# Phase one of a streaming hybrid layer: sigmoids held behind PSUM exits, z copied out of PSUM, B and C in a tile of their own

## The chip, the core and the metric

The kernel runs on one core of a Trainium2 chip, as one launch. The metric is the device time of an execution in microseconds; lower is better. The core has a matrix engine (PE, TensorE; its weight load is shown as PEld), a vector engine (DVE, VectorE), a scalar engine (ACT, ScalarE), a general one (POOL, GpSimd) and a queue that issues most DMAs (SP, SyncE). They run side by side, each in its own fixed order, and wait for each other through semaphores. Matmuls write into PSUM; the other engines read it from there, and a PSUM bank can only be written anew when its readers are done.

## What is computed

One inference step of one layer, for 2048 prompt tokens and 32 tokens of a running stream. The mixer reads a normalised input through one projection: half of its heads are stick-breaking attention, the other half a Mamba-2 SSD. Then come an output projection and a feed-forward network with a short convolution. The change is in the SSD side of the projection. Cut to that part:

```
# x: normalised input, 1024 wide; proj gives q, k, v (512 each), z (512), xBC (768), dt (8)
xBC, tail = causal_dwconv(xBC, prev, w, bias)      # 4 taps, 768 channels: x 512, B 128, C 128
xBC = xBC * sigmoid(xBC)                           # SiLU
y = ssd_scan(x, softplus(dt + b), a, B, C, h0) + D * x
y = rmsnorm(y * z * sigmoid(z), g)                 # gate, then norm
```

## The kernel before

Everything up to about 645 us is `phase_in`, which is called phase one here. It takes the tokens in four stretches `s` = 0 to 3 (512, 512, 512 and 544 tokens; the last one has the 32 stream tokens) and works with channels on the partitions. All projections are float32 products made of three matmuls: each operand is split in a high and a low half (`xhi`, `xlo`; a weight `w` is cast to its high half by ScalarE, L145, and GpSimd makes the low half, L146), and `dense` (L161) multiplies high by high, low by high and high by low for eight pieces of the input: 24 matmuls for a tile of 128 channels and up to 512 tokens. In s = 3 such a tile is two halves of 272 tokens. The results land in a PSUM tile `o` from a pool of two banks, which all projections of the phase share. So while one tile is being multiplied, the tile before it must be read out of the other bank, and a late exit stops TensorE.

One stretch runs like this:

- `split`: x, already scaled, gives `xhi` (ScalarE, L319) and `xlo` (VectorE, L320).
- Six convolution tiles `c` in the order 4 (B), 5 (C), 0, 1, 2, 3 (x). Each: 24 matmuls, a ScalarE copy from PSUM to `raw` (L377, L379 for the stream tokens), four VectorE operations (L384 and three times L388) into `xc`, a ScalarE sigmoid `t` (L392) and a VectorE product (L393). `xc` has one buffer, so this stretch's convolution can't start before the stretch before it is done with its own `xc`.
- The v tiles (L412): tokens in blocks of 128, for each block two halves of 24 matmuls with 260 columns, and a ScalarE copy out of each (L421; L419 in s = 0).
- Softplus and the SSD in blocks of 128 tokens: mask and decay in `acB` (VectorE, L488, L510; ScalarE exp, L492), the products with it on TensorE (L538), states `hT` (L562). B and C are operands of TensorE there (`cbm` comes from their product).
- `prep(s + 1)`: squares of the next x (ScalarE, L303 and L306; sums on GpSimd), its rstd (L248), and eight products on VectorE (L310), which scale it. k and q tiles.
- `gate`: four z tiles. In s = 1 and 2 a sigmoid `t` is read straight from PSUM (L627), VectorE multiplies PSUM by it (L628), which frees the bank, and multiplies `xc` by that (L630). In s = 0 a VectorE copy is made first; in s = 3 the gate runs later, spread over the attention.
- `gate_norm`: squares of `xc` (L641, L644), a sum over channels by a matmul `st` (L177), square root (ScalarE, L180), reciprocal (VectorE, L183), four products (L650), and the halves of the result, `khi` (ScalarE, L654) and `klo` (GpSimd, L656), which two DMAs each write out (L657, L658). The last `klo` is the last reader of `xc`.

No one writes the order of the engines by hand. The program is written in the order above, and a scheduler with a timeline of its own sets each engine's order from the dependencies, so an edit in one place can reorder its surroundings. Phase two is attention with the output projection, phase three the feed-forward network; the diff does not touch their code.

Of the kernel before, what the change touches and what calls it, by code (L numbers as in the profile page):

```python
# [8 lines left out]
F32 = mybir.dt.float32  # L9
F32R = mybir.dt.float32r  # L10
BF16 = mybir.dt.bfloat16
AF = mybir.ActivationFunctionType
ALU = mybir.AluOpType
# [18 lines left out]
P = 128  # L32
# [13 lines left out]
NSB = len(SBS)  # L46
# [19 lines left out]
def tiles_of(n):  # L66
    return [(0, n)] if n <= 512 else [(0, n // 2), (n // 2, n)]


class Kernel:  # L70
# [5 lines left out]
    def pin(self, mm):  # L76

        if self.anchor is not None:
            self.tc.add_manual_dep(
                mm.ins, self.anchor,  # L80
                mybir.DependencyInfo(mybir.DependencyClass.NoSync, mybir.DependencyReason.DATA),
                reason="pin",
            )

    def mark(self, mm):
        self.anchor = mm.ins.name
# [166 lines left out]
def phase_in(kn, ctx):  # L253
    nc, tc, a, o = kn.nc, kn.tc, kn.a, kn.o
# [5 lines left out]
    tmp = pool("in_tmp", 2)  # L260
# [94 lines left out]
    for s, (t0, nt) in enumerate(SBS):  # L355
        last = s == NSB - 1
        if s == 0:
            xs, r0 = first()
            rcol = kn.rcol
# [1 line left out]
            xs = split(s, nxt)  # L361
        xhi, xlo = xs
        raw = ep.tile([P, 6, 550], F32, name="raw")
        xc = kn.xcp.tile([P, 6, 547], F32, name="xc")
        W = 547 if last else 512
        nc.vector.tensor_copy(raw[:, :, 0:3], hist[:])
        if last:
            nc.vector.tensor_copy(
                raw[:, :, 515:518], kn.cv[:, C_SST : C_SST + 18].rearrange("p (c t) -> p c t", t=3)
            )  # L370
        for c in (4, 5, 0, 1, 2, 3):
            w = wfirst if s == 0 and c == 4 else kn.weight(wp, a["wbx"][c])
            for c0, c1 in tiles_of(nt):
                ps = psd.tile([P, 512], F32, name="o")
                kn.dense(ps, w, xs, c0, c1)
                e = min(c1, 512)
                nc.scalar.copy(raw[:, c, 3 + c0 : 3 + e], ps[:, : e - c0])  # L377
                if c1 > 512:
                    nc.scalar.copy(raw[:, c, 518:550], ps[:, e - c0 : c1 - c0])  # L379
            if s == 0:  # L380
                nc.vector.tensor_tensor(raw[:, c, 3 : 3 + nt], raw[:, c, 3 : 3 + nt], r0[:, :nt], op=ALU.mult)
            y = xc[:, c, :W]
            wc = C_SW + c * 4
            nc.vector.tensor_scalar(  # L384
                y, raw[:, c, 0:W], kn.col(wc), kn.col(C_SB + c), op0=ALU.mult, op1=ALU.add
            )
            for i in range(1, 4):
                nc.vector.scalar_tensor_tensor(  # L388
                    y, raw[:, c, i : i + W], kn.col(wc + i), y, op0=ALU.mult, op1=ALU.add
                )  # L390
            t = tmp.tile([P, 550], F32, name="t")
            nc.scalar.activation(t[:, :W], y, AF.Sigmoid)  # L392
            nc.vector.tensor_tensor(y, y, t[:, :W], op=ALU.mult)  # L393
        if last:
            nc.sync.dma_start(o["sconv"][0], raw[:, :, 512:515])
            nc.sync.dma_start(o["sconv"][1], raw[:, :, 547:550])
# [9 lines left out]
        for b in range(nb):  # L406
            q = min(P, nt - b * P)
            vp = [psd.tile([P, 512], F32, name="o") for _ in range(2)]
            for h in range(2):
                for k in range(KC):  # L410
                    for i, (l, rr) in enumerate(((xhi, wv[0]), (xlo, wv[0]), (xhi, wv[1]))):
                        nc.tensor.matmul(  # L412
                            vp[h][:q, :260], l[k][:, b * P : b * P + q], rr[:, k, h * 260 : h * 260 + 260],
                            start=i == 0 and k == 0, stop=i == 2 and k == KC - 1,
                        )
            v = sd.tile([P, 520], F32, name="v")
            for dst, src in ((v[:q, 0:260], vp[0][:q, :260]), (v[:q, 260:520], vp[1][:q, :260])):
                if s == 0:
                    nc.scalar.activation(dst, src, AF.Copy, scale=rcol[:q, b : b + 1])  # L419
                else:  # L420
                    nc.scalar.copy(dst, src)  # L421
            nc.vector.tensor_tensor(
                u[:q, b * 8 : b * 8 + 8], v[:q, 512:520], kn.cv[:q, C_DTB : C_DTB + 8], op=ALU.add
            )
            tok = t0 + b * P
            nc.sync.dma_start(o["v"][tok : tok + q, :], v[:q, :512])
            if b == 4:
                nc.sync.dma_start(kn.vF[:], v[:DEC, :512])
                continue
            vs = sd.tile([P, 2, 512], F32R, name="vs", bufs=1)  # L430
            nc.gpsimd.tensor_copy(vs[:, 0, :], v[:, :512])
            nc.gpsimd.tensor_tensor(vs[:, 1, :], v[:, :512], vs[:, 0, :].bitcast(F32), op=ALU.subtract)
            for e in range(2):
                nc.sync.dma_start(
                    kn.vS[s][:, :, b, e * DH : e * DH + DH].rearrange("h p d -> p h d"),
                    vs[:, e, :].bitcast(F32).rearrange("p (h d) -> p h d", d=DH),
                )
# [17 lines left out]
        ps = psm.tile([P, 512], F32, name="st")  # L455
# [10 lines left out]
        ps = psm.tile([P, 512], F32, name="st")  # L466
# [6 lines left out]
        for b in range(nb):  # L473
            q = min(P, nt - b * P)
            col0 = 515 if b == 4 else b * P
            sl = slice(col0, col0 + q)
# [17 lines left out]
            h_in = hS if b == 4 else hT[state["h"]]  # L494
            cy = psy.tile([P, 2, 512], F32, name="y")
            for g in range(2):
                rows = slice(g * 64, g * 64 + 64)
                nc.tensor.matmul(cy[:q, g, :q], xc[rows, 4, sl], xc[rows, 5, sl], start=True, stop=True)
                for i in range(2):
                    nc.tensor.matmul(  # L500
                        cy[:, g, P + i * q : P + i * q + q],
                        h_in[rows, 2 * i : 2 * i + 2, :].rearrange("p h d -> p (h d)"), xc[rows, 5, sl],
                        start=True, stop=True,
                    )
            cbm = sd.tile([P, 2, P], F32, name="cbm")
# [13 lines left out]
            ps = psm.tile([P, 512], F32, name="st")  # L519
# [9 lines left out]
                xw[:q], xdt[:q], te[:q, b * 8 : b * 8 + 8].unsqueeze(2).to_broadcast([q, NH, DH]), op=ALU.mult  # L529
            )  # L530
            ps = psm.tile([P, 512], F32, name="st")
            nc.tensor.transpose(ps[:q, :P], xc[:, 4, sl], kn.ident[:])
            bT = sd.tile([P, P], F32, name="bT")
            nc.scalar.copy(bT[:q, :], ps[:q, :P])
            yt = psy.tile([P, 2, 512], F32, name="y")
# [12 lines left out]
            ps = psm.tile([P, 512], F32, name="st")  # L548
# [6 lines left out]
            for g in range(2):  # L555
                rows = slice(g * 64, g * 64 + 64)
# [16 lines left out]
        for name, dst in (("wk", kn.kS), ("wq", kn.qS)):  # L573
            for c in range(4):
# [4 lines left out]
                for c0, c1 in tiles_of(nt):  # L579
                    ps = psd.tile([P, 512], F32, name="o")  # L580
                    kn.dense(ps, w, xs, c0, c1)
                    n = c1 - c0
# [13 lines left out]
        if last:  # L596
            return lambda tm, pool: (
                gate(kn, s, xs, xc, None, tm),
                gate_norm(kn, s, xc, tm, lambda sq, *r: kn.rstd_narrow(pool, *kn.bank, [sq], *r)),
            )  # L600
        bufs = {"khi": 2, "klo": 2, "t": 2, "sq": 1}
        tm = lambda nm: (so if nm in ("khi", "klo") else tmp).tile([P, 550 if nm == "t" else 544], F32, name=nm, bufs=bufs[nm])
        for _ in gate(kn, s, xs, xc, r0 if s == 0 else None, tm):
            pass
# [4 lines left out]
def gate(kn, s, xs, xc, r0, tm):  # L609

    nc, nt = kn.nc, SBS[s][1]
    tiles = tiles_of(nt)
    for c in range(4):
        w = kn.weight(kn.wp, kn.a["wz"][c])
        for c0, c1 in tiles:
            n = c1 - c0
            ps = kn.po.tile([P, 512], F32, name="o")
            for k in range(KC):
                kn.dense(ps, w[k : k + 1], xs, c0, c1, k0=k, first=k == 0, last=k == KC - 1, pin=s == NSB - 1)
                if len(tiles) == 1 or k % 2:  # L620
                    yield
            t = tm("t")
            if r0 is not None:
                z = tm("t")
                nc.vector.tensor_tensor(z[:, :n], ps[:, :n], r0[:, c0:c1], op=ALU.mult)
                ps = z
            nc.scalar.activation(t[:, :n], ps[:, :n], AF.Sigmoid)  # L627
            nc.vector.tensor_tensor(t[:, :n], ps[:, :n], t[:, :n], op=ALU.mult)  # L628
            e = min(c1, 512)
            nc.vector.tensor_tensor(xc[:, c, c0:e], xc[:, c, c0:e], t[:, : e - c0], op=ALU.mult)  # L630
            if c1 > 512:
                nc.gpsimd.tensor_tensor(xc[:, c, 512:544], xc[:, c, 515:547], t[:, e - c0 : n], op=ALU.mult)
# [839 lines left out]
def build(nc, tc, a, o):  # L1472
    kn = Kernel(nc, tc, a, o)
    with ExitStack() as ctx:
# [17 lines left out]
        with ExitStack() as c2:  # L1492
            kn.wp, kn.unit, kn.wbufs, kn.rbufs = c2.enter_context(tc.tile_pool(name="weights_in", bufs=1)), KC, 2, 2
            rest = phase_in(kn, c2)
# [125 lines left out]
```

## Time and profile before

| | |
|---|---|
| time, median of 3 runs | 2935.15 us (2931.43 to 2939.62) |
| profiled execution | 2941.02 us |
| its span | 2939.2 us, 46252 instructions |
| granted TensorE clock | 0.982 |
| busy | TensorE 96%, VectorE 58%, ScalarE 43%, GpSimd 43% |
| TensorE busy in 0 to 650 us | 593.75 us |

The span is the profiled part of the execution; 1.8 us lie around it. A busy share is an average over phases: what an edit in phase one can be worth is read from TensorE's waits there. In a row of the timeline the numbers are the start and the length in us, then engine, line, operation, output and inputs; the bracket at its end is the idle time before it and what ended it. In a row of groups they are the busy sum in us and the mean of one in ns.

### The profile page before, as it was taken

The numbers are of one execution on the slowest core, as the hardware profiler recorded it, in microseconds if no ns is written. First come the engines' busy times: TensorE is split into PE (matmuls) and PEld (weight loads), VectorE is DVE, ScalarE is ACT, GpSimd is POOL, SyncE is SP. The second block draws the span as 40 slices with busy tenths as digits, with TensorE's granted clock in tenths as the row PEclk, the third lists the DMA queues.
The fourth block names the chain that finished last, engine by engine and source line by source line (L and its number), as shares of the span: only waits on it lengthen the run. The fifth ranks groups of instructions, "written<-read, shape, count | busy, mean of one in ns | idle before, by whom it ended". The sixth has DMA issues, their size and how long they took to land.

```text
span 2939.2 us, 46252 instructions
## 1 busy us (share of the span) xinstructions
PE 2814.1 (96%) x16771; PEld 2427.5 (83%) x16771; DVE 1690.8 (58%) x2628; ACT 1263.4 (43%) x2622; POOL 1275.4 (43%) x1131
## 2 busy tenths in 40 slices
PE   7999999989889999999999999999999999999997
PEld 6777777977788888897788888977888889999997
DVE  7667586566773555447555556675666653623333
ACT  4344444337665555446333444654444443321111
POOL 4565555435766666656322323453223233511113
PEclk9999999989999999999999999999999999999999
DMA  5646464648787778777655556656555445765556
GB/s 179 183 137 193 132 176 124 174 115 271 247 282 263 253 263 276 266 256 250 215 180 172 174 180 219 225 182 205 176 172 170 160 159 202 241 181 179 170 178 200
DMA packets 333093, 586.47 MB, mean 200 GB/s; under 512 B 73306, under 2 KB 192738, under 8 KB 332866
## 3 DMA queue, kind: packets, MB, share of 16 engines
q1 hardware_dynamic: 332866, 583.52, 62.1%
q8 instruction: 134, 2.20, 0.3%
q14 instruction: 93, 0.76, 0.1%
HBM read 445.70 MB, written 137.69 MB: 198 GB/s over the span
## 4 chain that ended last, share of the span: by engine, by line
PE 72%; DVE 13%; DMA 7%; ACT 3%; issue 2%; POOL 1%; SPq 1%; DVEq 0%; ACTq 0%; POOLq 0%
PE o L161 35%; PE u L161 12%; PE t L161 10%; PE z L863 4%; PE pa L904 4%; PE pt L882 3%; DVE xc L388 2%; DMA acB<-acD 2%; PE o L412 1%; DVE acB L488 1%; DVE prow L714 1%; DMA xr<-hS 1%; DVE xc L384 1%; DVE xlo L320 1%; DVE x L310 1%
## 5 line engine op out<-in xcount | busy, mean ns | idle before, releaser
L161 PE MATMUL o<-xhi,w 128*128 128x512 f32 (+2 forms) x3968 | 1047.9, 346 | 24.1 <-ACT xhi L334 8.0
L161 PEld LDWEIGHTS o<-xhi,w 128*128 128x128 f32 x3968 | 697.3, 191 | 119.0 <-ACT xhi L334 8.0
L161 PE MATMUL o<-xlo,w 128*128 128x512 f32 (+2 forms) x1984 | 683.8, 345 | 6.3 <-DVE xlo L320 4.2
L146 POOL TENSOR_TENSOR w<-wraw,w 128x512 fp32r<-128x512 f32 (+3 forms) x244 | 384.3, 1577 | 261.4 <-ACT w L145 232.2
L719 POOL TENSOR_TENSOR beta<-beta,prow 128x512 f32<-128x512 f32 (+3 forms) x256 | 252.5, 987 | 442.7 <-DVE prow L714 366.8
L161 PEld LDWEIGHTS o<-xlo,w 128*128 128x128 f32 x1984 | 380.0, 192 | 50.4 <-DVE xlo L320 6.1
L161 PE MATMUL u<-xhi,w 128*128 128x512 f32 x1056 | 350.3, 398 | 0.0
L161 PE MATMUL o<-ah,w 128*128 128x512 f32 x992 | 344.4, 403 | 4.3 <-DVE f L1348 3.8
L1300 POOL TENSOR_TENSOR y<-y,gb 128x512 f32<-128x512 f32 (+1 forms) x88 | 116.0, 1318 | 503.2 <-ACT gb L1299 503.1
L714 DVE TENSOR_TENSOR_SCAN prow<-gam,prow,z 128x513 f32<-128x513 f32 x192 | 245.2, 1278 | 74.1 <-ACT beta L712 69.7
L887 DVE TENSOR_TENSOR wt<-pt,wt 128x512 fp32r<-128x512 f32 (+2 forms) x320 | 191.0, 602 | 159.6 <-ACT wt L886 157.8
L886 ACT CAST wt<-pt 128x512 fp32r<-128x512 f32 (+2 forms) x320 | 166.9, 527 | 218.2 <-PE pt L882 216.3
L145 ACT CAST w<-wraw 128x512 fp32r<-128x512 f32 (+3 forms) x244 | 172.1, 705 | 170.6 <-PE o L161 98.6
L161 PEld LDWEIGHTS u<-xhi,w 128*128 128x128 f32 x1056 | 199.1, 189 | 46.8
L161 PEld LDWEIGHTS o<-ah,w 128*128 128x128 f32 x992 | 187.2, 189 | 47.0 <-DVE f L1348 6.0
L711 ACT ACTIVATE gam<-z 128x512 f32<-128x512 f32 (+2 forms) x320 | 172.3, 538 | 96.0 <-PE z L863 53.9
L161 PE MATMUL u<-xlo,w 128*128 128x512 f32 x528 | 209.5, 397 | 0.0
L161 PE MATMUL o<-al,w 128*128 128x512 f32 x496 | 196.7, 397 | 0.0
L161 PE MATMUL t<-xhi,w 128*128 128x272 f32 x960 | 189.6, 293 | 2.6 <-DMA w<-wS_up 1.7
L882 PE MATMUL pt<-ident,beta 128*128 128x128 f32 x1088 | 180.3, 277 | 4.2 <-DVE wt L887 2.7
L1292 DVE SCALAR_TENSOR_TENSOR y<-gb,cv,y 128x512 f32<-128x512 f32 (+1 forms) x176 | 142.4, 809 | 72.6 <-ACT y L1290 69.9
L904 PE MATMUL pa<-wt,v 128*64 128x256 f32 (+3 forms) x1152 | 172.3, 280 | 8.6 <-DVE wt L887 6.6
(275 smaller groups left out, 4956.4 us busy)
## 6 DMA issues: line engine op xcount, KB each, us to landing
w<-wS_up SPq DMA_DIRECT2D x264, 512.0 KB, 3.6
w<-wS_dn SPq DMA_DIRECT2D x144, 384.0 KB, 3.5
wS_up<-w SPq DMA_DIRECT2D x88, 512.0 KB, 3.4
w<-wS_out SPq DMA_DIRECT2D x78, 512.0 KB, 5.7
wraw<-wup SPq DMA_DIRECT2D x88, 256.0 KB, 4.0
k<-kS SPq DMA_DIRECT2D x80, 256.0 KB, 4.1
v<-vS SPq DMA_DIRECT2D x80, 256.0 KB, 3.8
wS_dn<-w SPq DMA_DIRECT2D x48, 384.0 KB, 3.1
```

What stands on the lines that cost most here:

```text
L145: nc.scalar.copy(hi, raw[:, :m, :])
L146: nc.gpsimd.tensor_tensor(lo, raw[:, :m, :], hi.bitcast(F32), op=ALU.subtract)
L161: mm = nc.tensor.matmul(ps[:, : c1 - c0], l, r, start=first and i == 0 and k == 0, stop=last and i == 2 and k == len(w) - 1, **({"skip_gro ...
L711: nc.scalar.activation(g[:, c0:512], z, AF.Sigmoid, scale=-0.125)
L714: nc.vector.tensor_tensor_scan(back(pr), back(g), z[:, 0:1].to_broadcast([P, n + 1]), self.kn.ones[:, 0:1] if prev is None else prev, op0= ...
L719: eng.tensor_tensor(b[:, :n], b[:, :n], pr[:, c0 + 1 : 513], op=ALU.mult)
L863: mm = nc.tensor.matmul(z[:, :n], q[:, P * b : P * b + P], k[:, :n], start=e == 0, stop=e == 1 and kc < s)
L882: mm = nc.tensor.transpose(t[:, P * j : P * j + P], w[:, P * j : P * j + P], kn.ident[:])
L886: nc.scalar.copy(hi, t)
L887: nc.vector.tensor_tensor(lo, t, hi.bitcast(F32), op=ALU.subtract)
L904: nc.tensor.matmul(av[:m, 2 * P * p + c0 : 2 * P * p + 2 * P], v[:, j, :m], wt[:, rest, j, c0:], start=kc == s and p + j + rest == 0, stop ...
L1292: nc.vector.scalar_tensor_tensor(y[:, :W], gb[:, i : i + W], kn.col(wc + i), y[:, :W], op0=ALU.mult, op1=ALU.add)
```

## The change

Lines in the new kernel are 8 to 22 higher. There are three edits, all in phase one.

1. A helper `behind` adds a dependency that sets order alone, without a semaphore. The sigmoid and product of a convolution tile are no longer issued with it but owed, and put behind the PSUM copy of the next tile; those of the last tile (c = 3) behind the v copy of block 0.
2. In s = 1 and 2 z is copied from PSUM into a new tile `zc` (two buffers) by ScalarE. Sigmoid and product read `zc`: eight more ScalarE copies.
3. B and C go into a tile `bc` of their own with its own buffer; `xc` keeps the four x tiles.

```diff
+    def behind(self, inst, other):
+        self.tc.add_manual_dep(
+            inst.ins, other.ins.name,
+            mybir.DependencyInfo(mybir.DependencyClass.NoSync, mybir.DependencyReason.DATA),
+            reason="behind",
+        )
...
-        xc = kn.xcp.tile([P, 6, 547], F32, name="xc")
+        xc = kn.xcp.tile([P, 4, 547], F32, name="xc")
+        bc = kn.xcp.tile([P, 2, 547], F32, name="bc")
...
+        owed = None
+        def silu(y, copy):
+            t = tmp.tile([P, 550], F32, name="t")
+            kn.behind(nc.scalar.activation(t[:, :W], y, AF.Sigmoid), copy)
+            nc.vector.tensor_tensor(y, y, t[:, :W], op=ALU.mult)
...
-            y = xc[:, c, :W]
+            y = xc[:, c, :W] if c < 4 else bc[:, c - 4, :W]
...
-            t = tmp.tile([P, 550], F32, name="t")
-            nc.scalar.activation(t[:, :W], y, AF.Sigmoid)
-            nc.vector.tensor_tensor(y, y, t[:, :W], op=ALU.mult)
+            if owed is not None:
+                silu(owed, copy)
+            owed = y
...
+            if b == 0:
+                silu(owed, copy)
...
-                nc.tensor.matmul(cy[:q, g, :q], xc[rows, 4, sl], xc[rows, 5, sl], start=True, stop=True)
+                nc.tensor.matmul(cy[:q, g, :q], bc[rows, 0, sl], bc[rows, 1, sl], start=True, stop=True)
...
+            elif s < NSB - 1:
+                z = tm("zc")
+                nc.scalar.copy(z[:, :n], ps[:, :n])
+                ps = z
             nc.scalar.activation(t[:, :n], ps[:, :n], AF.Sigmoid)
             nc.vector.tensor_tensor(t[:, :n], ps[:, :n], t[:, :n], op=ALU.mult)
```

ScalarE, v tiles of s = 2, before (`v` copies, sigmoids of `xc`, and the squares `t<-x` of the next x):

```order
L421 COPY v_3223<-o_3173 128x260
L421 COPY v_3223<-o_3174 128x260
L392 ACTIVATE t_2978<-xc_2941 128x512
L392 ACTIVATE t_3016<-xc_2941 128x512
L421 COPY v_3283<-o_3233 128x260
L421 COPY v_3283<-o_3234 128x260
L392 ACTIVATE t_3054<-xc_2941 128x512
L392 ACTIVATE t_3092<-xc_2941 128x512
L421 COPY v_3343<-o_3293 128x260
```

and after:

```order
L437 COPY v_3231<-o_3181 128x260
L384 ACTIVATE t_3100<-xc_2951 128x512
L384 ACTIVATE t_3138<-xc_2951 128x512
L437 COPY v_3231<-o_3182 128x260
L384 ACTIVATE t_3176<-xc_2951 128x512
L437 COPY v_3294<-o_3244 128x260
L384 ACTIVATE t_3234<-xc_2951 128x512
L314 ACTIVATE t_3711<-x_3704 128x544
L314 ACTIVATE t_3714<-x_3704 128x544
L437 COPY v_3294<-o_3245 128x260
```

B's and C's sigmoids have left this place, and those of the x tiles stand singly between the first four v copies, with two squares ahead of the fourth.

ScalarE, z tiles of s = 1, before (`t<-o` is a z sigmoid, `w` a weight cast, `sq` the first square of the gate norm):

```order
L248 COPY rstd_2390<-st_2389 128x512
L627 ACTIVATE t_2758<-o_2733 128x512
L145 CAST w_2798<-wraw_2796 128x1024
L627 ACTIVATE t_2792<-o_2767 128x512
L145 CAST w_2832<-wraw_2830 128x1024
L641 ACTIVATE sq_2864<-xc_1601 128x512
L627 ACTIVATE t_2826<-o_2801 128x512
```

and after:

```order
L256 COPY rstd_2392<-st_2391 128x512
L647 COPY zc_2761<-o_2735 128x512
L153 CAST w_2804<-wraw_2802 128x1024
L649 ACTIVATE t_2760<-zc_2761 128x512
L663 ACTIVATE sq_2874<-xc_1602 128x512
L647 COPY zc_2797<-o_2771 128x512
L153 CAST w_2840<-wraw_2838 128x1024
L649 ACTIVATE t_2796<-zc_2797 128x512
L647 COPY zc_2833<-o_2807 128x512
```

The copies to `zc` have come in, and the square of `xc` now stands ahead of the second of them and of the fourth tile's weight cast.

TensorE, the sum `st` of the gate norm of s = 1, among the matmuls of the next stretch's third convolution tile (c = 0), before:

```order
L161 MATMUL o_2986<-xhi7_2915,w_2983 128x512
L161 MATMUL o_3024<-xhi0_2908,w_3021 128x512
L161 MATMUL o_3024<-xlo0_2916,w_3021 128x512
L177 MATMUL st_2876<-sq_2864,ones_72 128x512
L161 MATMUL o_3024<-xhi1_2909,w_3021 128x512
```

and after:

```order
L169 MATMUL o_3032<-xhi0_2918,w_3029 128x512
L169 MATMUL o_3032<-xhi7_2925,w_3029 128x512
L185 MATMUL st_2886<-sq_2874,ones_72 128x512
L169 MATMUL o_3032<-xlo7_2933,w_3029 128x512
L169 MATMUL o_3070<-xhi0_2918,w_3067 128x512
```

It stood behind 2 of the tile's 24 matmuls and now stands behind 22 (rows between are left out). For s = 2 it stood in the middle of the tile c = 5's second half and now stands at the end of the first half of c = 0, 35 matmuls of 272 tokens later. On VectorE of s = 2 the convolution of `bc` now stands ahead of the gate norm's reciprocal, and its two products on either side of it.

In s = 0 ScalarE and TensorE keep their order. In the SSD of s = 1 the second block's product with `acB` stands 4 matmuls of a projection tile behind the first block's; before, 21 stood between them. In s = 2 the eight products that scale the next x stand behind the gate's products of the second z tile instead of the first.

More of the change, by code (lines that the diff above doesn't have):

```diff
@@ L376, in phase_in @@
                 e = min(c1, 512)
-                nc.scalar.copy(raw[:, c, 3 + c0 : 3 + e], ps[:, : e - c0])
+                copy = nc.scalar.copy(raw[:, c, 3 + c0 : 3 + e], ps[:, : e - c0])
                 if c1 > 512:
-                    nc.scalar.copy(raw[:, c, 518:550], ps[:, e - c0 : c1 - c0])
+                    copy = nc.scalar.copy(raw[:, c, 518:550], ps[:, e - c0 : c1 - c0])
             if s == 0:
                 nc.vector.tensor_tensor(raw[:, c, 3 : 3 + nt], raw[:, c, 3 : 3 + nt], r0[:, :nt], op=ALU.mult)
-            y = xc[:, c, :W]
+            y = xc[:, c, :W] if c < 4 else bc[:, c - 4, :W]
             wc = C_SW + c * 4
@@ L418, in phase_in @@
                 if s == 0:
-                    nc.scalar.activation(dst, src, AF.Copy, scale=rcol[:q, b : b + 1])
+                    copy = nc.scalar.activation(dst, src, AF.Copy, scale=rcol[:q, b : b + 1])
                 else:
-                    nc.scalar.copy(dst, src)
+                    copy = nc.scalar.copy(dst, src)
+            if b == 0:
+                silu(owed, copy)
             nc.vector.tensor_tensor(
@@ L501, in phase_in @@
                         cy[:, g, P + i * q : P + i * q + q],
-                        h_in[rows, 2 * i : 2 * i + 2, :].rearrange("p h d -> p (h d)"), xc[rows, 5, sl],
+                        h_in[rows, 2 * i : 2 * i + 2, :].rearrange("p h d -> p (h d)"), bc[rows, 1, sl],
                         start=True, stop=True,
@@ L531, in phase_in @@
             ps = psm.tile([P, 512], F32, name="st")
-            nc.tensor.transpose(ps[:q, :P], xc[:, 4, sl], kn.ident[:])
+            nc.tensor.transpose(ps[:q, :P], bc[:, 0, sl], kn.ident[:])
             bT = sd.tile([P, P], F32, name="bT")
@@ L600, in phase_in @@
             )
-        bufs = {"khi": 2, "klo": 2, "t": 2, "sq": 1}
+        bufs = {"khi": 2, "klo": 2, "t": 2, "sq": 1, "zc": 2}
         tm = lambda nm: (so if nm in ("khi", "klo") else tmp).tile([P, 550 if nm == "t" else 544], F32, name=nm, bufs=bufs[nm])
```

## Prediction

> **What bounds the kernel now.** I read the page's busy line and its chain first, then the busy time by stage, then TensorE's waits in phase one, then the rows around each wait.
>
> ```profile
> PE 2814.1 (96%) x16771; PEld 2427.5 (83%) x16771; DVE 1690.8 (58%) x2628; ACT 1263.4 (43%) x2622; POOL 1275.4 (43%) x1131
> PE 72%; DVE 13%; DMA 7%; ACT 3%; issue 2%; POOL 1%; SPq 1%; DVEq 0%; ACTq 0%; POOLq 0%
> 0.00:650.00 650.00, 593.75 (x3519) 496.17 (x3519) 428.75 (x713) 272.02 (x435) 331.58 (x208) 0.97 0.54 158
> PE o L412 <- ACT v L421: 8.9, 3, 3.4
> PE o L161 <- DVE t L628: 5.1, 2, 2.6
> PE o L161 <- ACT raw L377: 1.4, 1, 1.4
> PE o L412 <- ACT raw L379: 0.9, 1, 0.9
> ```
>
> The first line is busy time by engine: TensorE is busy 96% of the span, so only its idle time can be won. The second is the chain that ended last, by engine. The third is phase one, 0 to 650 us (length, then busy time of TensorE, its weight load, VectorE, ScalarE, GpSimd, granted clock, DMA share, GB/s): TensorE is idle 56 us. The last four are waits of TensorE there (total, times, longest) for a PSUM bank that ScalarE or VectorE empties too late, all in s = 1, 2 and 3: 8.9 + 5.1 + 1.4 + 0.9 = 16.3 us. The other 40 us are SSD, input and weight waits and s = 0, whose order on ScalarE and TensorE is the same before and after.
>
> **The v tiles (edit 1).** First TensorE's v waits in s = 1, 2, 3, two of its matmuls that follow each other freely, and the ScalarE row behind the second wait; then VectorE's convolution, where it starts and what an operation takes.
>
> ```profile
> 224.95 0.39 PE L412 MATMUL o<-wvhi,xhi 128*128 128x260 f32 x1 [2.88 <-ACT v L421]
> 386.07 0.39 PE L412 MATMUL o<-wvhi,xhi 128*128 128x260 f32 x1 [3.43 <-ACT v L421]
> 544.76 0.58 PE L412 MATMUL o<-wvhi,xhi 128*128 128x260 f32 x1 [2.58 <-ACT v L421]
> 378.07 0.28 PE L412 MATMUL o<-wvlo,xhi 128*128 128x260 f32 x1
> 378.19 0.28 PE L412 MATMUL o<-wvhi,xhi 128*128 128x260 f32 x1
> 384.46 1.29 ACT L392 ACTIVATE t<-xc 128x512 f32<-128x512 f32 x2 [5.83 <-DVE xc L388]
> 207.49 4.44 DVE L384 TENSOR_SCALAR xc<-raw,cv 128x512 f32<-128x512 f32 x5 [5.64 <-POOL klo L656]
> 368.64 4.43 DVE L384 TENSOR_SCALAR xc<-raw,cv 128x512 f32<-128x512 f32 x5 [7.12 <-POOL klo L656]
> 517.73 4.07 DVE L384 TENSOR_SCALAR xc<-raw,cv 128x547 f32<-128x547 f32 x4 [5.65 <-POOL klo L656]
> L388 DVE SCALAR_TENSOR_TENSOR xc<-raw,cv,xc 128x512 f32<-128x512 f32 x18 | 15.8, 935 | 0.0
> L393 DVE TENSOR_TENSOR xc<-xc,t 128x512 f32<-128x512 f32 x6 | 5.0, 866 | 0.0
> L377 ACT COPY raw<-o 128x512 f32<-128x512 f32 x6 | 3.5, 584 | 12.3 <-PE o L161 12.3
> ```
>
> A v copy stands behind two sigmoids, and those wait for the convolution, which starts only when the last `klo` of the stretch before gives `xc` free: call these starts T0 (207.5, 368.6, 517.7). After the edits B and C need no T0, and of the rest each sigmoid stands behind one v copy: copy 1, sigmoids of c = 0 and 1, copy 2, sigmoid of 2, copy 3, sigmoid of 3, two squares, copy 4. By the rows an operation is 0.9 us; c = 1 is done after 10 to 14 operations (I take T0 + 10), c = 3 after 16 and three products (T0 + 17). With 0.65 us for a sigmoid or a square (1.29 for two) and 0.6 for a copy (a raw copy's 584 ns), copy 2 lands at T0 + 11.3, copy 3 at T0 + 14.2, copy 4 at T0 + 19.6. TensorE, which has 2 banks, asks for copy 2, 3, 4 at intervals of 2.86 us (24 matmuls, 0.12 us from start to start as in the rows at 378).
>
> T0 itself moves, since B's and C's products now stand between the reciprocal and the gate norm's products, and the norm's sum stands later on TensorE:
>
> ```profile
> 344.00 0.40 PE L161 MATMUL o<-xlo,w 128*128 128x512 f32 x1
> 344.70 0.40 PE L161 MATMUL o<-xlo,w 128*128 128x512 f32 x1
> 347.73 0.59 PE L177 MATMUL st<-sq,ones 128*128 128x512 f32 x1
> 352.32 3.35 DVE L183 RECIPROCAL rstd<-rstd 128x512 f32<-128x512 f32 x1 [12.23 <-ACT rstd L180]
> 502.08 1.02 PE L177 MATMUL st<-sq,ones 128*128 128x512 f32 x2
> 503.14 0.69 ACT L180 ACTIVATE rstd<-st,eps 128x512 f32<-128x512 f32 x1 [0.67 <-PE st L177]
> ```
>
> - s = 1: the sum stays; one product more, 1.3 us, ahead of the norm's. T0 208.8. Copy 2 at 220.1 against a demand at 219.2 (two halves ahead of the wait's start at 222.07, less one): 0.9. Copy 4 at 228.4 against 225.8: 2.6. Together 3.5 against 2.88: **−0.6**.
> - s = 2: the sum moves back by 20 matmuls, 20 x 0.235 = 4.7 us (from the row at 344.00 to that at 344.70 run three), to 352.4. The square root, 0.7 us ahead of the reciprocal at 352.32, began 2.9 us after the sum was done; with this slack and C's sigmoid and product the norm's products start 2.6 us later. T0 371.2. Copy 2 at 382.5 against 379.8: 2.7. Copy 4 at 390.8 against 388.2: 2.6. Together 5.3 against 3.43: **−1.9**.
> - s = 3: the sum moves back by 35 matmuls of 272 columns (some 0.12 us each, like v's of 260), 4.2 us, with no slack behind it (the square root at 503.14 waited for it); C's sigmoid then waits for the next raw copies, and T0 comes 6.9 us later, 524.6. Copy 1 now stands behind the sigmoids of c = 0 and 1 and lands at 536.1 against 534.2; copy 3 at 542.9 against 541.9. Together 2.9 against 2.58 + 0.91: +0.6; with half of a slow stretch (below) **+1.4**.
>
> The bounds of edit 1 for the three: all waits gone, 2.88 + 3.43 + 2.58 + 0.91 = 9.8 us gained; T0 4 us later still in each, 12 us lost.
>
> **z through zc (edit 2).**
>
> ```profile
> 318.59 0.48 PE L161 MATMUL o<-xhi,w 128*128 128x512 f32 x1 [2.64 <-DVE t L628]
> 484.04 0.47 PE L161 MATMUL o<-xhi,w 128*128 128x512 f32 x1 [2.48 <-DVE t L628]
> 310.30 7.54 DVE L310 SCALAR_TENSOR_TENSOR x<-x,cv,rstd 128x512 f32<-128x512 f32 x8 [0.45 <-ACT rstd L248]
> 320.11 1.05 PE L161 MATMUL o<-xhi,w 128*128 128x512 f32 x2
> 323.49 0.64 PE L161 MATMUL o<-xhi,w 128*128 128x512 f32 x2
> 474.98 8.31 DVE L310 SCALAR_TENSOR_TENSOR x<-x,cv,rstd 128x544 f32<-128x544 f32 x8 [1.55 <-ACT rstd L246]
> 487.38 4.53 DVE L320 TENSOR_TENSOR xlo<-x,xhi 128x544 fp32r<-128x544 f32 x7
> 320.66 0.63 ACT L641 ACTIVATE sq<-xc 128x512 f32<-128x512 f32 x1 [3.14 <-DVE xc L630]
> L145 ACT CAST w<-wraw 128x1024 fp32r<-128x1024 f32 x29 | 30.5, 1052 | 6.9 <-DMA wraw<-wq 5.7 <-DMA wraw<-wbx 1.2
> L146 POOL TENSOR_TENSOR w<-wraw,w 128x1024 fp32r<-128x1024 f32 x29 | 73.7, 2541 | 63.6 <-ACT w L145 61.0 <-DMA eA<-acD 1.7 <-POOL klo L656 0.9
> L628 DVE TENSOR_TENSOR t<-o,t 128x512 f32<-128x512 f32 x8 | 5.4, 681 | 14.9 <-ACT t L627 14.9
> L630 DVE TENSOR_TENSOR xc<-xc,t 128x512 f32<-128x512 f32 x8 | 10.1, 1275 | 0.1
> ```
>
> In s = 1 the third z tile waits 2.64 us, because the product that frees the bank stands behind eight products of the next stretch's x. The copy to `zc` frees it at once. After this wait the rows at 320.11 and 323.49 show the price of an idle TensorE: two matmuls 1.05 us, then 0.64, about 3.4 us at half pace, 1.7 us lost (the row behind the v wait of s = 3 is slow too, 0.58 us against 0.39 in s = 1 and 2). Gained: 2.6 + 1.7 = 4.3. But the square of `xc` now stands ahead of the second `zc` copy and of the weight cast of the fourth tile. It can start when the products behind x are done (317.8 + 0.7 + 1.3 = 319.8), so square 320.4, copy 321.0, cast 322.1, GpSimd's low half 324.6; TensorE, no longer held, needs that half at 322.3. The new wait is 2.0 to 2.6. I take 4.3 − 2.0 = **+2.3**, with ends 0.6 (the new wait also brings a slow stretch) and 4.3.
>
> The Trainium skill, "SBUF — State Buffer", section "Who interferes with whom", says that a VectorE instruction with two SBUF inputs contends with a GpSimd instruction that reads SBUF, and one with at most one such input does not. The last two rows agree: one PSUM input 681 ns, two SBUF inputs 1275 ns, the same shape. Since the eight products of z now read `zc`, by this rule each would take 0.6 us longer, the square would come at 321.0 and this term would be +1.7 instead of +2.3.
>
> In s = 2 the copy wins 2.48 us, but x's products (474.98) now stand behind two tiles of z, whose second is done by TensorE some 4 us after them: they start at about 479.5, and the low halves, before at 487.4, follow at 489, so that the next stretch's first matmul waits about 1.6 us. With the 1.4 us raw wait shortened a little: **+0.7** (ends −2.0 and +2.5). The eight copies cost ScalarE 8 x 0.58 us, a raw copy's time, beside an engine that is 43% busy: nothing on the path except where they are counted above.
>
> **B and C apart (edit 3).** Their convolution fills VectorE's 12 us before the reciprocal (row at 352.32): no cost there but T0's, counted. In s = 1 the SSD of the second block now stands 4 matmuls of the dense tiles behind the first block's, before 21, so less covers its mask product:
>
> ```profile
> 275.13 1.84 DVE L510 TENSOR_TENSOR acB<-acB,cbm 128x512 f32<-128x512 f32 x2
> 277.40 1.09 PE L538 MATMUL y<-acB,xdt 128*64 128x128 f32 x16
> ```
>
> It is ready at 277.0, just ahead of its reader; drawn 17 matmuls (4.0 us) forward TensorE would wait about 3, and gets about half back later: **−1.4** (ends −3.0 and 0).
>
> **Sum.** −0.6 − 1.9 + 1.4 + 2.3 + 0.7 − 1.4 = +0.5 us gained. The profiled execution took 2941.0 us (span 2939.2), 5.9 over the median of 2935.15: 2940.5 there, 2934.6 against the median. The order of the later phases shifts too in places; no row prices that, and I let it stand as zero with 4 us to either side, about as far as the runs shown lie from their median.
>
> **The rivals.** A change of 0.3%, 8.8 us, is about what a measurement of this kernel can tell from none.
>
> *All waits go.* If T0 stays where it is and the square does not hold the cast, 9.8 + 2.6 us of waits and two slow stretches of 1.7 vanish, less 1.4: 14.4 us, 2920.7. For it: the waits are real and a copy is short. Against it: the sums of the gate norm stand later, and T0 decides the sigmoids.
>
> *T0 comes later still.* The one release that the three v regions hang on is the last `klo`; between gate norm and `klo` stand weight products of 2.5 us on GpSimd. Each us that T0 is later than worked out delays copies 2 to 4 by one in three stretches: from 3.1 us on the kernel is measurably slower, at 4 us by 12 − 0.5 = 11.5 us, 2946.6. Against it: `klo` and products alternate already.
>
> *The sigmoids were not what held v.* If the copies wait as long behind other work (squares, raw copies), nothing moves: 2935.2.
>
> **How the numbers follow.** Waits change place, within 5 us: 0.46, nearly all within 0.3%. All waits go: 0.24, faster. T0 later still: 0.22, slower. Nothing moves: 0.08. So faster 0.26 with a little of the first case, within 0.3% 0.52, slower 0.22. The likeliest case alone spans 2929 to 2940. The range takes in the first rival less 3 us for the runs' spread, 2918, and the second, 2947.
>
> **What would show it.** In the trace after: T0 of s = 2 and 3 at 2 to 7 us later relative to the v tiles; two v waits a stretch, at copies 2 and 4, in place of one of 3; no wait for z's product but one for GpSimd's low half in s = 1; a wait for `acB` in the second block of s = 1. It is wrong if the v waits are gone (the convolution was early enough), or if T0 is late by more than 3 us beyond this.

## The result

The changed kernel takes 2962.14 us (median of 4 runs, 2958.91 to 2971.91), the kernel before 2935.71 (4 runs beside them, 2931.43 to 2939.62). The ratio is 1.0097 (95% interval 1.0073 to 1.0121): about 28 us slower, where 2934.6 in a range of 2918 to 2947 was forecast. First the busy line and the chain of the page after, then phase one and 1300 to 1460 us by stage (columns as in the prediction), then TensorE's waits up to 700 us.

```profile
PE 2818.4 (95%) x16771; PEld 2435.9 (82%) x16771; DVE 1714.4 (58%) x2628; ACT 1268.0 (43%) x2630; POOL 1282.6 (43%) x1131
PE 67%; DVE 4%; DMA 3%; ACT 1%; issue 1%; POOL 1%; SPq 0%; DVEq 0%; POOLq 0%; ACTq 0%
0.00:650.00 650.00, 591.48 (x3487) 497.70 (x3488) 451.61 (x709) 272.14 (x434) 337.76 (x207) 0.96 0.53 157
1300.00:1460.00 160.00, 144.43 (x904) 127.24 (x903) 99.78 (x154) 78.82 (x194) 84.87 (x96) 0.96 0.67 214
PE o L428 <- ACT v L437: 13.6, 4, 5.6
PE y L556 <- DVE acB L528: 7.9, 5, 2.7
PE o L169 <- POOL w L154: 6.2, 9, 1.4
PE o L169 <- ACT w L153: 2.4, 1, 2.4
```

The span grew by 19.0 us, to 2958.2. TensorE is 4.3 us busier with the same matmuls (granted clock 0.977, before 0.982) and idle for 14.7 us more. z's product is gone from the list, as forecast. The v copies cost 13.6 us instead of 8.9, weights 8.6 instead of 1.9. The rows behind the v waits, and the start of the convolution of `xc`, called T0, with what it waited for:

```profile
227.55 0.59 PE L428 MATMUL o<-wvhi,xhi 128*128 128x260 f32 x1 [5.45 <-ACT v L437]
386.20 0.59 PE L428 MATMUL o<-wvhi,xhi 128*128 128x260 f32 x1 [5.56 <-ACT v L437]
546.42 0.39 PE L428 MATMUL o<-wvhi,xhi 128*128 128x260 f32 x1 [0.75 <-ACT v L437]
551.38 0.39 PE L428 MATMUL o<-wvhi,xhi 128*128 128x260 f32 x1 [1.84 <-ACT v L437]
213.80 1.29 POOL L678 TENSOR_TENSOR klo<-xc,khi 128x512 fp32r<-128x512 f32 x1 [3.63 <-DMA yS<-klo]
215.13 5.61 DVE L400 TENSOR_SCALAR xc<-raw,cv 128x512 f32<-128x512 f32 x3 [8.99 <-POOL klo L678]
372.45 1.30 POOL L678 TENSOR_TENSOR klo<-xc,khi 128x512 fp32r<-128x512 f32 x1 [3.66 <-DMA yS<-klo]
532.21 3.71 DVE L400 TENSOR_SCALAR xc<-raw,cv 128x547 f32<-128x547 f32 x3 [8.05 <-POOL klo L678]
```

In s = 1 and 2 one long wait stands where two shorter ones were worked out, and the last `klo` waits 3.6 us for the store of an earlier one, which in the trace before had cost 0.5 us at most:

```profile
367.32 1.28 POOL L656 TENSOR_TENSOR klo<-xc,khi 128x512 fp32r<-128x512 f32 x1 [0.52 <-DMA yS<-klo]
```

Why it waits now can be read from GpSimd's order ahead of it, here in front of s = 1, before and then after:

```profile
199.55 3.25 POOL L656 TENSOR_TENSOR klo<-xc,khi 128x512 fp32r<-128x512 f32 x2 [1.28 <-ACT khi L654]
202.77 2.41 POOL L146 TENSOR_TENSOR w<-wraw,w 128x1024 fp32r<-128x1024 f32 x1
```

```profile
203.51 1.75 POOL L678 TENSOR_TENSOR klo<-xc,khi 128x512 fp32r<-128x512 f32 x1 [1.28 <-ACT khi L676]
205.22 2.85 POOL L154 TENSOR_TENSOR w<-wraw,w 128x1024 fp32r<-128x1024 f32 x1
208.04 2.13 POOL L678 TENSOR_TENSOR klo<-xc,khi 128x512 fp32r<-128x512 f32 x2
```

`klo` has two buffers, so the fourth and last one needs the store of the second. Before, a weight product stood behind the second `klo` and gave its store time; now it stands ahead of it. The store of the second is issued only at 209.15; the fourth could start at 210.2 and starts at 213.8.

And in code that the diff does not touch, two of the waits of TensorE in the changed kernel are 3.5 and 5.4 us long, where the longest one of the kernel before between 860 and 2939 us is 3.5 (at 1414):

```profile
1385.15 0.50 PE L169 MATMUL o<-ah,w 128*128 128x512 f32 x1 [3.54 <-DVE f L1370]
1438.86 0.80 PE L885 MATMUL z<-k,qa 128*128 128x512 f32 x1 [5.35 <-DVE rn_v L228]
```

### The profile page after: what moved, and what is told of

Its sections match the earlier page's. It is cut to its first block, busy times and chain, and to the rows that moved or that the text cites. A ratio compares the mean times of both kernels' runs of the same rounds, so it can differ in the third digit from the quotient of the medians.

```text
span 2958.2 us, 46253 instructions
## 1 busy us (share of the span) xinstructions
PE 2818.4 (95%) x16771; PEld 2435.9 (82%) x16771; DVE 1714.4 (58%) x2628; ACT 1268.0 (43%) x2630; POOL 1282.6 (43%) x1131
## 4 chain that ended last, share of the span: by engine, by line
PE 67%; DVE 4%; DMA 3%; ACT 1%; issue 1%; POOL 1%; SPq 0%; DVEq 0%; POOLq 0%; ACTq 0%
PE o L169 31%; PE u L169 12%; PE t L169 11%; PE z L885 4%; PE pa L926 4%; PE pt L904 4%; DVE prow L736 1%; DVE xlo L1074 1%; DMA xr<-hS 1%; DMA w<-wS_out 1%; PE u L211 1%; DMA w<-wS_up 0%; PE u L246 0%; DMA xhi<-yS 0%; DVE f L1402 0%
## 5 line engine op out<-in xcount | busy, mean ns | idle before, releaser
L154 POOL TENSOR_TENSOR w<-wraw,w 128x512 fp32r<-128x512 f32 (+3 forms) x244 | 391.2, 1606 | 278.0 <-ACT w L153 254.6
```

Source lines behind the costliest of these rows:

```text
L154: nc.gpsimd.tensor_tensor(lo, raw[:, :m, :], hi.bitcast(F32), op=ALU.subtract)
```

## The experiments

Two tools serve all of them. All variants write the same instructions behind phase one in the same sequence, so the order in which the scheduler put them for one kernel can be laid on another: dependencies of order alone, as in `behind`, chain each engine's instructions from a table. "Old order" is that of the kernel before, "new order" that of the changed kernel. "The rest" is everything behind phase one.

```diff
+    em = list(nc.cur_bb.bb.instructions)
...
+    for d in flat:                       # a table of places, engine by engine
...
+        i = em[at]
+        if prev is not None:
+            tc.add_manual_dep(
+                i, prev.name,
+                mybir.DependencyInfo(mybir.DependencyClass.NoSync, mybir.DependencyReason.DATA),
+                reason="order",
+            )
+        prev = i
```

Medians of different runs are not compared; each ratio is to the kernel before on the same chip, with its 95% interval.

### Where: phase one or the rest

The changed kernel with the rest in the old order; the kernel before with the rest in the new order.

> The changed kernel, but from attention on each engine takes its instructions in the order of the kernel before; phase one keeps the changed order. Theory 'two places': by the traces TensorE is some 7 to 11 us late at the end of phase one and loses another 8 to 15 us later, in code that the diff does not touch, because its order was reshuffled. Then this kernel is 7 to 11 us over before (2943 to 2947). Rival 'carried on': the rest is slow because phase one hands its data over late; then the order of the rest does not matter and this stays 19 to 28 us over before (2955 to 2964). Rival 'only the rest': phase one's loss is made up by slack; then within 4 us of before.

> The kernel before, with none of the three edits, but from attention on in the order of the changed kernel. Theory 'two places': 10 to 17 us over before (2946 to 2953), with the waits of the changed kernel at the end of the first feed-forward stretch (1385 and 1439 us there). Rival 'carried on': within 4 us of before. Rival 'only the rest': 20 to 28 us over before.

Measured: 1.0029 (1.0016 to 1.0042), 8 us over, and 1.0052 (1.0033 to 1.0071), 15 us over. "Two places" holds: 15 us are lost without any of the edits, and the two add up to 24 of 28 us. "Carried on" and "only the rest" fall.

The new order of the rest differs from the old one only up to about 1460 us. Two kernels divide that at 860 us: the kernel before with a table that is new in one part and old in the other.

> The kernel before, with the changed kernel's order only in the stretch of the program that ran from about 860 to 1460 us (attention of the second stretch and the feed-forward network of the first); outside it its own order. The new order in all of the rest cost 0.52%, 15 us, without any edit. Theory 'one place': the waits for a square root chain and for f at about 1370, 1423 and 1427 us (3.6, 4.8 and 2.1 us, with slow stretches behind) are the loss: 9 to 16 us slower than before. Rival 'the start of attention': within 4 us of before.

> The complement: the kernel before with the changed kernel's order only from the end of phase one to about 860 us; all orders behind 1460 us are the same in both kernels. Theory 'one place': within 4 us of before. Rival 'the start of attention': 10 to 16 us slower.

Measured: 1.0050 (1.0032 to 1.0069) and 1.0010 (0.9997 to 1.0023). The loss is in the later part; the 3 us of the earlier part can't be told from zero. First 1300 to 1460 us by stage, of the kernel before and then of this one (e13); then VectorE and TensorE of e13 around its longest wait there.

```profile
1300.00:1460.00 160.00, 151.43 (x900) 130.43 (x899) 99.41 (x155) 80.18 (x195) 81.45 (x91) 0.99 0.71 229
```

```profile
1300.00:1460.00 160.00, 142.58 (x886) 125.08 (x885) 99.32 (x153) 76.44 (x189) 82.36 (x91) 0.96 0.66 211
1428.52 0.42 DVE L1384 TENSOR_TENSOR f<-f,xr 128x256 f32<-128x256 f32 x1 [5.55 <-DMA xr<-hS]
1433.43 1.50 DVE L1384 TENSOR_TENSOR f<-f,xr 128x256 f32<-128x256 f32 x1 [3.89 <-DMA xr<-hS]
1436.77 0.79 PE L863 MATMUL z<-k,qa 128*128 128x512 f32 x1 [6.57 <-DVE rn_v L220]
```

TensorE loses 8.9 us of busy time and runs at a clock of 0.96 instead of 0.99 there. VectorE stands in order behind two additions that wait 5.6 and 3.9 us for the load of `xr`, and what TensorE waits for (`rn_v`) stands behind them. In the kernel before two such additions stand ahead of `rn_v` as well:

```profile
1409.03 0.42 DVE L1384 TENSOR_TENSOR f<-f,xr 128x256 f32<-128x256 f32 x1 [2.00 <-DMA xr<-hS]
1412.89 0.43 DVE L1384 TENSOR_TENSOR f<-f,xr 128x256 f32<-128x256 f32 x1 [2.83 <-DMA xr<-hS]
1413.24 0.15 DVE L220 SCALAR_TENSOR_TENSOR rn_v<-u,rcol 128x2 f32<-128x2 f32 x1
```

They wait 2.0 and 2.8 us there. So the same chain is 4.6 us longer in the new order. TensorE's waits for `rn_v` and for `f` in this stage, before and then in e13:

```profile
PE u L238 <- POOL rn_v L226: 3.5, 1, 3.5
PE o L161 <- DVE f L1348: 1.8, 2, 1.0
```

```profile
PE z L863 <- DVE rn_v L220: 6.6, 1, 6.6
PE o L161 <- DVE f L1348: 4.7, 3, 3.5
```

`f` empties a bank of the feed-forward network; in the new order it stands on VectorE behind four low halves (`xlo`, 3.95 us from 1376.78 on). `rn_v` (3.1 us more), `f` (2.9) and a third group, `wt` (from 0.9 to 3.5), make up 8.6 of the 9 us. Why the loads of `xr` come later was not tried, and the other 6 of the 15 us were not taken apart.

### Which edit, in the scheduler's order of phase one

Each edit alone, the rest in the old order.

```diff
 e3: only behind() and silu()        (xc with six tiles, z from PSUM)
 e4: only z = tm("zc"); nc.scalar.copy(z[:, :n], ps[:, :n])
 e5: only bc = kn.xcp.tile([P, 2, 547], F32, name="bc")
```

> Edit 1 alone (sigmoids behind the next PSUM exit), the rest of the kernel in the order of before. Theory 'release decides': xc comes free as early as before, c = 0 and 1 wait for it, and the v waits only change place: within 4 us of before. Rival 'sigmoids were the wait': v waits gone, 6 to 10 us faster. Rival 'edit 1 is the loss': the v waits grow as in the changed kernel and it is 5 to 9 us slower.

> Edit 2 alone (z through zc in s = 1 and 2), the rest of the kernel in the order of before. Theory 'weights late': the two z waits of 2.6 and 2.5 us go, and waits for GpSimd's low half of the weights come in their place, because casts now stand behind copies and squares; between 3 us faster and 5 us slower. Rival 'plain win': 4 to 7 us faster. Rival 'edit 2 is the loss': 6 to 11 us slower.

> Edit 3 alone (B and C in their own tile), the rest of the kernel in the order of before. Edit 1 alone gave nothing and edit 2 alone a gain, so if the edits add up this one must lose some 15 us in phase one. Theory 'release late': B's and C's convolution and products get ahead of the gate norm, xc comes free 3 to 5 us later relative to the v tiles in s = 1 and 2, and the v waits of the kernel before grow from 2.9 and 3.4 to 5 to 7 us: 6 to 15 us slower. Rival 'only together': alone it does nothing (within 4 us), since without the owed sigmoids the order around the gate norm stays.

Measured: 1.0004 (0.9990 to 1.0017), 0.9977 (0.9960 to 0.9995) and 1.0041 (1.0026 to 1.0055). Edit 1 does nothing alone: the old order already has each sigmoid behind the next exit (the three edits fit into it as it is, below). Edit 2 gains 7 us, edit 3 loses 12. But the v waits of edit 3 alone did not grow, as "release late" had it:

```profile
PE o L428 <- ACT v L437: 6.8, 3, 3.3
PE o L169 <- POOL w L154: 6.2, 8, 1.4
PE st L548 <- DVE hT L578: 7.0, 3, 3.4
```

In its trace weights wait 4.3 us more than before and states 2.4 more, v 2.1 less; where the rest of the 12 us lies was not taken apart. That miss asks whether it is the tile or the order.

### The edits in the old order

The same edits with every engine in the old order in phase one too; a zc copy stands directly ahead of its sigmoid.

> All three edits, but every engine takes its instructions in the order of the kernel before, in phase one too; the eight zc copies stand each directly ahead of its sigmoid. Theory 'order': the edits themselves cost nothing, the 26 us are the orders that the scheduler made of them; the two z waits (5.1 us) go, with one slow stretch of 1.7: 3 to 9 us under before. Rival 'edits cost': B and C in their own tile or the products with two SBUF inputs cost by themselves, and it stays 5 us or more over before.

> Edit 2 alone in the order of before in both phases. Theory 'order': the same as the three edits in that order within 3 us, 3 to 9 us under before, since edits 1 and 3 then change nothing. Rival 'the gain of edit 2 alone (0.23%) came from its reordering': within 3 us of before.

> Edit 3 alone in the order of before in both phases; only the place of B and C in memory and what they wait for differs. It was 0.41% slower in the scheduler's order. Theory 'order': within 4 us of before. Rival 'the tile itself': 8 to 14 us slower as before.

Measured: 1.0001 (0.9985 to 1.0017), 1.0016 (1.0003 to 1.0028), 1.0000 (0.9984 to 1.0016). The three edits as such cost nothing, and B and C in a tile of their own cost nothing, to within some 5 us: the 28 us are order. (e10 lies 5 us over, with an interval of 1 to 8; e9 has the same copies and does not.) They gain nothing either, against what I expected of the z copies. In e10 TensorE no longer waits for z's product; its wait list for x's low halves, two of the rows, and what VectorE and GpSimd do there:

```profile
PE o L169 <- DVE xlo L328: 9.7, 8, 2.1
486.33 0.39 PE L169 MATMUL o<-xlo,w 128*128 128x272 f32 x1 [1.88 <-DVE xlo L328]
491.48 0.59 PE L169 MATMUL o<-xlo,w 128*128 128x272 f32 x1 [2.15 <-DVE xlo L328]
485.56 8.85 DVE L328 TENSOR_TENSOR xlo<-x,xhi 128x544 fp32r<-128x544 f32 x7
488.01 2.83 POOL L154 TENSOR_TENSOR w<-wraw,w 128x1024 fp32r<-128x1024 f32 x1
```

The 5.1 us come back as 5.5 us more of waiting for `xlo` (4.2 before; 4.6 more in e9), at the start of the next stretch. There are two reasons in the rows. x's products on VectorE end no earlier, counted from the first product of z, so TensorE, early at z, is early at x too. And in front of s = 3 seven low halves take 8.85 us, in e9 too, where they took 4.53 before: GpSimd, idle from 485.6 to 491.1 in the kernel before, now has a sum of squares and a weight product beside them. That the two hold each other up is read from these rows, not tested. The gain of edit 2 alone in the scheduler's order came with a reordering around it.

### The release of xc

Two buffers for `xc` take the wait for the stretch before away: for the three edits, for edit 2, for the kernel before, and for edits 1 and 2, each with the rest in the old order. The scheduler orders phase one anew in each.

```diff
-        kn.xcp = ssd.enter_context(tc.tile_pool(name="ssd_out", bufs=1, reuse_waits="tile", side="right"))
+        kn.xcp = ssd.enter_context(tc.tile_pool(name="ssd_out", bufs=2, reuse_waits="tile", side="right"))
```

> The three edits, the rest in the order of before, and xc and bc with two buffers, so that a stretch's convolution never waits for the stretch before it. Theory 'release decides': the v waits (14.4 us in four places with one buffer) fall to under 4 us, and instead of 8 us over before it is 3 to 10 us under before. Rival 'weights and order': the late weight halves and the SSD are the loss; the v waits shrink, but it stays 2 to 8 us over before.

> Edit 2 alone, which gave 0.23%, with two buffers for xc, the rest in the order of before. Theory 'release decides': v waits of 8.7 us and the slow stretches behind them go as well: 10 to 18 us under before, the fastest so far. Rival: the convolution, now early, takes VectorE from x's products and SSD, and it is no better than edit 2 alone (5 to 9 us under).

> The kernel before with two buffers for xc and none of the edits, the rest in its own order. Theory 'release decides': the v waits of 8.9 us in s = 1, 2, 3 go, with two slow stretches of 1.7 us: 6 to 12 us under before. Rival: v copies still stand behind sigmoids that the scheduler puts ahead of them: within 4 us of before.

> Edits 1 and 2 with two buffers for xc, the rest in the order of before. With two buffers and without edit 1 the sigmoids got ahead of the raw copies, and those waits (13 us) took the place of the v waits. Theory 'edit 1 needs an early release': with the sigmoids held behind the exits neither raw nor v copies are waited for long: 8 to 16 us under before, the fastest. Rival: another wait takes their place (x's low halves, weights): within 5 us of before.

Measured: 1.0002 (0.9986 to 1.0019), 1.0034 (1.0020 to 1.0049), 1.0005 (0.9988 to 1.0022), 1.0009 (0.9994 to 1.0023). With the three edits it won back the 8 us of phase one, but none of the four is faster than before, and none came out as its theory had it: in e8 and e12 the rival's small change held, in e6 and e7 neither did. One row of waits each of e6, e7 and e8:

```profile
PE o L428 <- ACT v L437: 4.0, 3, 1.9
```

```profile
PE o L427 <- ACT raw L392: 13.2, 5, 4.9
```

```profile
PE o L412 <- ACT raw L377: 12.2, 5, 4.1
```

With edit 1 the v waits fell from 14.4 us to 4.0. Without it the early convolution let the sigmoids get ahead of the raw copies, and TensorE waited for those instead. e12, which is e7 with edit 1, waits 1.7 us in that row where e7 waits 13.2. That is the one place where `behind` did something. Since these four change the order too, the last test keeps it: as e1, every engine's order the same, but four buffers for `khi` and `klo`.

```diff
-        bufs = {"khi": 2, "klo": 2, "t": 2, "sq": 1, "zc": 2}
+        bufs = {"khi": 4, "klo": 4, "t": 2, "sq": 1, "zc": 2}
```

> As the three edits with the old order of the rest (0.29% over before), every engine's order exactly as there; only khi and klo have four buffers, not two, so that the last klo no longer waits for the DMA of an earlier one (3.6 us in s = 1 and 2 of the changed kernel). Theory 'release decides': xc comes free some 3.5 us earlier in s = 1 and 2, the v waits of 5.5 us there fall to 2 to 3, and it is 4 to 9 us faster than with two buffers, that is within 4 us of before. Rival: the release waits for GpSimd anyway (weights ahead of klo), and it stays 6 to 11 us over before.

Measured: 1.0001 (0.9988 to 1.0013). In the order that cost 8 us the whole loss is gone. Rows of e1, then of e15:

```profile
371.49 1.29 POOL L678 TENSOR_TENSOR klo<-xc,khi 128x512 fp32r<-128x512 f32 x1 [4.15 <-DMA yS<-klo]
385.24 0.59 PE L428 MATMUL o<-wvhi,xhi 128*128 128x260 f32 x1 [6.07 <-ACT v L437]
PE o L428 <- ACT v L437: 14.4, 4, 6.1
```

```profile
366.28 3.52 DVE L400 TENSOR_SCALAR xc<-raw,cv 128x512 f32<-128x512 f32 x3 [5.32 <-POOL klo L678]
378.76 0.39 PE L428 MATMUL o<-wvhi,xhi 128*128 128x260 f32 x1 [1.83 <-ACT v L437]
PE o L428 <- ACT v L437: 5.6, 4, 1.8
```

The last `klo` no longer waits for a store, and T0 stands 1.9 us ahead of the start of the v tiles in s = 1 and 2, where in e1 it stood 1.1 and 2.4 us behind. The v waits fall by 8.8 us and the time by 8. In phase one the wait for the stores was the loss (`khi` got its buffers along with `klo`, so the two are not told apart). Weights still wait 8.3 us in e15, 6.4 more than before; that the time is that of before goes with z's 5.1 us and some of the v waits being won.

### A faster version

Edit 2 alone once more with more rounds (e16), the same with four buffers for `khi` and `klo` (e17), and the kernel before with those buffers (e18), every engine's order kept.

> Edit 2 alone in the scheduler's order for phase one, the old order in the rest, as in the run that was 0.23% under before (interval 0.05 to 0.40), with more rounds: the version that beats both kernels so far. Theory 'a real gain by order': 4 to 10 us under before again. Rival 'chance': within 3 us, like the same edit in the old order.

> The version that was 0.15 to 0.23% under before (zc alone, scheduler's order in phase one, old order in the rest) with four buffers for khi and klo, every engine's order as there. Theory 'release decides': xc comes free some us earlier, v waits of 8.7 us fall to 4 or less: 0.3 to 0.6% under before, the fastest. Rival: its last klo hardly waits for its store, and it stays 0.1 to 0.25% under.

> The kernel before with four buffers for khi and klo and nothing else, in its own order. In its trace the last klo waits 0.5 us for a store, so T0 comes little earlier: within 4 us of before by the theory 'release decides'. Rival: more buffers gain as much as under the changed order (8 us), whatever the klo waits for.

Measured: 0.9985 (0.9972 to 0.9997), 0.9970 (0.9956 to 0.9984), 1.0003 (0.9988 to 1.0017). e17 beats both kernels: 9 us under the one before, 37 under the changed one by the two ratios. Its v waits fell from 9.8 us in e16 to 6.9, not to 4 as expected (first e16, then e17), and its interval overlaps that of e16, so what the buffers add there is not settled. In the order of before they add nothing: the last `klo` hardly waited there.

```profile
PE o L427 <- ACT v L436: 9.8, 4, 4.1
```

```profile
PE o L427 <- ACT v L436: 6.9, 4, 2.9
```

## Why the prediction was wrong

- *The rest as zero, 4 us to either side.* This step failed most. It measured 15 us. No row of the trace before priced it, as the text said, but the bound was taken from the runs' spread, which says nothing on a new order. The trace before had a chain there with no slack (the two additions ahead of `rn_v`, with TensorE waiting 3.5 us at its end), and the change moved it; I looked at TensorE's waits in phase one alone.
- *T0.* I added C's product and the later sum to a release chain that I took as fixed. For s = 1 and 2 that gave 1.7 us ahead of the v tiles' start and 0.2 behind it; measured 1.8 and 1.9 behind (215.13 and 373.79 against starts at 213.36 and 371.89). What was missing is the double-buffered `klo` and its store: 3.6 us in each. In s = 1 that is the whole miss: without it, in e15, T0 is 1.9 us ahead. In s = 2 it is more than the miss: in e15 T0 is 1.9 us ahead there too, so the part of the chain that I did work out was some 2 us too long, and the two errors partly cancel. For s = 3 the 6.9 us were right (4.4 us ahead of the start of v at 536.63; 4.0 worked out).
- *The v copies.* The mechanism was right: waits change place and follow T0. I worked out 11.7 us of waits in the three against 9.8 before (the raw wait of s = 3 counted in), that is −1.9, or −1.1 with half of a slow stretch less; measured were 13.6, that is −3.8. With the store's wait taken away it turned to a gain of 4.2 us (5.6), so the term's size hung on T0.
- *z.* The 2.0 us of a new wait for the low half did not come in that size: weights waited 0.5 us at 328 us. The largest new wait for a weight, 2.4 us, is in the k and q tiles of s = 1, where I had not looked; in s = 2 the wait for x's low half, worked out at 1.6, measured 2.8 (492.41). The port rule of the Trainium skill ("SBUF — State Buffer", section "Who interferes with whom") bears out in these rows:

```profile
L650 DVE TENSOR_TENSOR t<-zc,t 128x512 f32<-128x512 f32 x8 | 11.6, 1446 | 15.1 <-ACT t L649 15.1
L652 DVE TENSOR_TENSOR xc<-xc,t 128x512 f32<-128x512 f32 x8 | 9.6, 1206 | 0.2
```

  The product of z took 681 ns with one input in PSUM and takes 1446 with both in SBUF, 6 us of VectorE for eight (0.8 us each on average, where 0.6 was given by the rule): 680 ns where GpSimd stood idle (at 322.07), 2.46 us beside a weight product (at 326.13). In e15 they take 1445 ns too and the time is that of before, so no cost of theirs shows.
- *SSD.* Forecast −1.4 us. The wait for `acB` came where it was forecast, at the second block of s = 1, but it was 1.0 us long (at 279.22), and a wait of 1.0 us at the third block (289.97 before) went. The sum up to 700 us went from 5.1 to 7.9, but with phase one untouched it is 4.6 in e14 and 7.3 in e2, so no loss can be read from it.
- *The rival "T0 later still"* named the direction and the release behind a third of the loss at 0.22. What I held against it, that `klo` and weight products alternate already, is what failed: before they stood two `klo`, a product, two `klo`, and once the product stood ahead of the second `klo`, its store came too late for the last one. Its price was that of phase one alone, so the 15 us of the rest lay outside the range.

## What to carry to other kernels

Where a scheduler sets the order, an edit's price has two parts, the edit and the order made of it; lay the old order on the new code and the new order on the old code, and the two parts stand apart. Here the edits were worth nothing and the orders 28 us. When a buffer's release decides, follow it to its last reader and ask what that reader waits for: two more buffers for each of two staging tiles gave back 8 us that looked like a matter of sigmoids and copies.

## What was not expected

A wait of TensorE that is removed can come back whole: 5.1 us of z waits turned into 5.5 us more of `xlo` waits at the start of the next stretch (e10), where x's low halves, now beside GpSimd's work, took 8.85 us instead of 4.53. And edits in phase one, 0 to 650 us, changed the order of code that runs at 860 to 1460 us, and that alone cost 15 us (e13), more than all that they did in phase one.
